# Two-block transformer forward on one Trainium2 core: bias and forget tables on GpSimd's DMA queue, query weights loaded ahead of the compressed branch's, first squares on ScalarE, output tiles j and j+4 in one PSUM bank

## The chip, the cores and the metric

The kernel runs as one program on one core of a Trainium2 chip. The metric is the device time of one execution in microseconds (us), as the median of several runs. TensorE (PE) multiplies, its weight loads (PEld) overlap with it; VectorE (DVE) and ScalarE (ACT) work element by element and empty PSUM; GpSimd (POOL) does small sums and reciprocal roots; SyncE (SP) issues most DMA transfers. DMA transfers can also be issued from POOL's own instruction stream, where they stand in line with its other instructions.

## What is computed

A sequence of 256 positions with 1,024 channels goes through two layers and then a second block of three stages, all in float32.

```
h = x
h = h + moba_nsa_mixer(rmsnorm(h))      # layer 0: dense causal heads with relative bias, and three-branch heads
h = h + sqrelu_mlp(rmsnorm(h))          # 1024 -> 4096 -> 1024
h = h + fox_mixer(rmsnorm(h))           # layer 1: 16 heads, forget gates
h = h + sqrelu_mlp(rmsnorm(h))
h = rmsnorm(h)
n = modulate(rmsnorm(h)); h = h + 0.5*gt1*swiglu(n)     # 2816 hidden
n = modulate(rmsnorm(h)); h = h + gt2*hybrid_mixer(n)   # pooling (4 windows) and dilated attention (8 heads)
n = modulate(rmsnorm(h)); h = h + 0.5*gt3*swiglu(n)
out = rmsnorm(h)

fox_mixer:  q, k, v, fz = split(h @ w_in);  log_f = log_sigmoid(fz + b_forget);  cum = cumsum(log_f over positions)
            s = q k^T * scale + cum[query] - cum[key];  p = causal softmax(s);  out = (p v) @ w_out
moba_nsa:   in 8 heads s = q k^T * scale + table[bucket(distance)], causal softmax, p v
            in 8 heads the same bias with three branches: compressed keys (silu(blocks @ w1) @ w2), selected, window
```

## The kernel before

Activations are held transposed: `Ht` is 128 partitions x 8 channel tiles x 256 positions. Float32 precision is kept by splitting each operand into a rounded high part and a remainder, so every product is three matmuls (`mm3`, lines 403 to 405: high x high, high weight x low activation, low weight x high activation). The activations' parts are `nh` and `nl`, the weights' `wh` and `wl`. A "product" below is one such group of three on a 128 x 128 weight tile.

**Weights.** `specs` lists all weight pieces (most are 1 MB) in the order in which they are loaded. They go into a ring of five raw buffers (`raw`): piece i+5 is loaded when piece i has been split. The split is done by halves, the high part by an ACT copy (L276, for the first piece L287) and the low part by a DVE subtraction (L282, first piece L288), into rings of five (`wh`, `wl`). Pieces of the compressed branch (`cmp`) are used as they are loaded. All these loads, the 786 KB write of the relative-bias table to DRAM (`vd`) and the eight reads of the table back from there (`hh<-vd`, 256 KB each, four for each of the tables `T[1]` and `T[0]`) stand in SP's stream one behind the other, through `queue()`, which keeps their order.

**Order of the work.** The kernel is written as a stream of projections. At certain points `poke()` runs one step of side work: hooks set with `later(n, f)` (f runs n pokes on), generators for attention (`quad`: scores `s` L749, bias and row minimum on DVE L759/L760, exponentials on ACT L761/L763, scaling on DVE L775/L776, transposes `t` on PE L783, their copy on ACT L785, products with v into `o` L807/L810), the splits of coming weights, and the modulation's row sums. `settle(key)` steps until the generators pushed under a key are done. Each engine then runs its instructions strictly in the order that comes out of this, so one that waits holds up all behind it on its engine.

**Norms.** Each stage begins projecting before its norm is known; the reciprocal root follows in three steps set by `norm_begin(eps, n1, n2)`: at poke n1 the sums of squares are reduced on PE (`ss`), at n2 the diagonal matrix is made, at n2+1 PE spreads it (`r`).

**First norm.** The squares of the input's eight tiles are summed by `first_squares`: for half of them POOL squares and adds (L533, L542, L547), for the other half ACT squares (L539) and DVE adds.

**Fox mixer.** The chunks of four heads come in the order c = 3, 2, 1, 0, each with projections fv, fq, fk. `forget` (in chunk 3) makes log_f, transposes it on PE (`a` L1304), sums it along the positions (DVE L1307), writes it to DRAM (`cd`, POOL L1310) and reads it back into all partitions in four parts for four heads each (`hh<-cd`, POOL L1312); then POOL adds the causal mask to the four parts (L1316), and for each head POOL adds it once more to a half (`pre`, L1339).

**Output projections.** `out_proj` and the second half of `ffn` collect eight output tiles of 128 x 256 in four PSUM banks, two tiles in each bank. Tiles 2t and 2t+1 share a bank:

```
ps = acc[t]                                  # ffn
mm3(ps[:, jj * S:(jj + 1) * S], ...)         # tile 2t+jj
ps = acc[2 * c + jj // 2]                    # out_proj, tile 4c+jj
```

When a tile is finished, DVE adds it to `Ht` (L868 in the first two mixers, L942/L943 in the MLPs, L1449 in the gated MLPs, L1551 in the hybrid mixer), and the next stage's `nh`, `nl` are made of it. During the last pair of tiles `state["hold"]` keeps the splits of coming weights back.

**Hybrid mixer.** v is transposed on PE by `v_trans` (`a` L1523), the pooled groups come from `pool_gen` (a chain of DVE additions L1492 to L1498, then `a` L1503 on PE); both are generators with fixed delays in pokes.

Of the kernel before, what the change touches and what calls it, by code (L numbers as in the profile page):

```python
# [19 lines left out]
P = 128  # L20
S = 256
# [47 lines left out]
def tile_two_blocks(ctx, tc, a, out):  # L69
# [166 lines left out]
    cap = [5]  # L236
# [84 lines left out]

    def take(name):
        i = state["next"]
        state["next"] += 1
        assert specs[i][0] == name, (specs[i][0], name)
        return Weights(i)
# [128 lines left out]
    def late_loads():  # L455
        for h in range(2):
            queue(w2k[:, :, 64 * h:64 * h + 64], rows(a["cmp_k_w2"], 0, 2))
        queue(w2v, rows(a["cmp_v_w2"], 0, 2))
# [68 lines left out]
    def first_squares(t):  # L527
        x = [Ht[:, 2 * t + j, :] for j in range(2)]
        if t < 2:
            eng = gp_  # L530
            sq = sb([P, 512], F32, "sq")
            for j in range(2):
                eng.tensor_tensor(sq[:, j * S:(j + 1) * S], x[j], x[j], OP.mult)  # L533
        else:
            eng = dve
            sq = sb([P, 512], F32, "ev", 3)
            with tc.issue_after(state["conva"]):
                for j in range(2):
                    act.activation(sq[:, j * S:(j + 1) * S], x[j], AF.Square)  # L539
        if t % 2 == 0:  # L540
            acc = sb([P, S], F32, ("ssq", "nv")[t // 2])
            eng.tensor_tensor(acc, sq[:, :S], sq[:, S:], OP.add)  # L542
            cur.setdefault("ssq", []).append(acc)
        else:
            acc = cur["ssq"][-1]
            for j in range(2):
                eng.tensor_tensor(acc, acc, sq[:, j * S:(j + 1) * S], OP.add)  # L547
# [270 lines left out]
    def out_proj(name, oh, ol, k0, swap, done):  # L818
        acc = [None] * 4

        def part(c, k0, first):
# [6 lines left out]
            def product(jj, h):  # L828
                ps = acc[2 * c + jj // 2]
                s = slice(jj * P, (jj + 1) * P)  # L830
                for i, k in enumerate(order[h]):
                    st = first and h == 0 and i == 0 and jj % 2 == 0
                    mm3(ps[:, jj % 2 * S:(jj % 2 + 1) * S], w.h(2 * h + i, s), w.l(2 * h + i, s), oh[:, k0 + k, :],
                        ol[:, k0 + k, :], st, not first and h == 1 and i == 1, skip_group_check=True)

            def out(jj):
                ps = acc[2 * c + jj // 2]
                done(4 * c + jj, ps[:, jj % 2 * S:(jj % 2 + 1) * S])
                if jj % 2:
# [21 lines left out]
        for c in range(2):  # L861
            part(c, k0, True)
        settle("o")
# [7 lines left out]
    def ffn(tag, n, up, done, hold=True):  # L871
# [3 lines left out]
        for i in range(len(bl) + 1):  # L875
# [10 lines left out]
            for t in range(4):  # L886
                w = take(tag + "2")
                if b == 0:
                    acc[t] = bank("acc")
                ps = acc[t]  # L890
                end = b == len(bl) - 1
                def part(jj, ks):
                    s = slice(jj * P, (jj + 1) * P)
                    for k in ks:
                        mm3(ps[:, jj * S:(jj + 1) * S], w.h(k, s), w.l(k, s), hh[:, k, :], hl[:, k, :],
                            b == 0 and jj == 0 and k == 0, end and k == m - 1, skip_group_check=True)
                    poke()
                if end and t == 3:
                    state["hold"] = hold
                    ks = [w.half(h) for h in range(2)]  # L900
                    for jj in range(2):
                        for x in ks:
                            part(jj, x)
                        done(2 * t + jj, ps[:, jj * S:(jj + 1) * S])
                    drop(ps)
# [5 lines left out]
                if end:  # L911
                    for j in range(2):
                        done(2 * t + j, ps[:, j * S:(j + 1) * S])
                    drop(ps)
# [72 lines left out]
    def body():  # L987
# [297 lines left out]
        norm_begin(1e-5, 4, 7)  # L1285
# [3 lines left out]
        def forget(ps):  # L1289
# [11 lines left out]
            yield 3  # L1301
            p = bank("a")
# [11 lines left out]
            for x in (3, 2, 1, 0):  # L1314
                part = cumb[x // 2][:, 4 * (x % 2):4 * (x % 2) + 4, P:S]
                gp_.tensor_tensor(part, part, tri[:, None, :].to_broadcast([P, 4, P]), OP.add)  # L1316
        oh_ = sb([P, KT, 258], F32R, "nh", 2)[:, :, :S]
        ol_ = sb([P, KT, 258], F32R, "nl", 2)[:, :, :S]
        for c in (3, 2, 1, 0):
            first = c == 3  # L1320
            q, k, v = qkv()
            if first:
                ps_v = gemm_nat_more("fv")

# [3 lines left out]
                on_norm(put_v)  # L1328
                ps_q = gemm_pair("fq")
                on_norm(lambda: evac_q(ps_q, q))  # L1330
            else:
                evac_v(gemm_nat("fv"), v)
                evac_q(gemm_pair("fq"), q)
            evac_k(gemm_pair("fk"), k)
            bts = {}

            def pre(j, e, t, c=c, bts=bts):
# [3 lines left out]
            push("o" if c < 2 else "f", quad(  # L1341
                q, lambda j, e, k=k: k[64 * e:64 * e + 64, j, :],
                lambda j, e, b, v=v: v[:, b, 128 * j + 64 * e:128 * j + 64 * e + 64],
                lambda j, e, bts=bts: bts[j, e],
                None, Out(oh_, ol_, 2 * c), True, pre, quick=c == 0), None)
        settle("f")
        new_n()
        out_proj("fout", oh_, ol_, 4, True, lagged(gain["mlp1"], add_h))
# [136 lines left out]
        def pool_gen(gi, u):  # L1485
# [13 lines left out]
            yield 2  # L1499
# [27 lines left out]
        for c in range(2):  # L1527
# [18 lines left out]
            on_norm(attend)  # L1546
# [99 lines left out]
```

## Time and profile before

| what | value |
|---|---|
| median of three runs | 1148.22 us (1147.53 to 1151.86) |
| the profiled execution, its own time | 1150.76 us |
| its span in the trace | 1149.0 us |
| PE busy | 1095.1 us, 95% of the span, 9,088 matmuls |
| PEld busy | 1064.0 us (93%) |
| DVE busy | 805.9 us (70%) |
| ACT busy | 577.1 us (50%) |
| POOL busy | 112.2 us (10%) |
| moved by DMA | 233.72 MB, mean 203 GB/s |

The shares are means over stages with different limits. A row of the timeline gives start, duration, engine, line, operation, output and inputs and, in brackets, how long the engine had been idle before and what released it. Matmuls overlap in the pipeline, so a matmul's own duration (0.28 us) is longer than the distance to the next one.

### The profile page before, as it was taken

How to read it: one execution, taken by the hardware profiler on the slowest of the kernel's cores; microseconds unless marked ns; L12 is line 12 of the kernel's file. 1: busy time of each engine (PE TensorE's matmuls, PEld its weight loads, DVE VectorE, ACT ScalarE, POOL GpSimd, SP SyncE). 2: the span in 40 equal slices, each digit the busy share in tenths (PEclk: the TensorE clock that was granted, in tenths of full speed). 3: DMA queues.
4: the chain of work that ended last, by engine and by line, in shares of the span. 5: the costliest groups of instructions: out<-in, count | busy, mean ns of one | idle time of the engine just before them, and what ended most of it. 6: DMA issues, size and time to landing. Idle time of an engine off the chain costs nothing.

```text
span 1149.0 us, 22404 instructions
## 1 busy us (share of the span) xinstructions
PE 1095.1 (95%) x9088; PEld 1064.0 (93%) x9088; DVE 805.9 (70%) x1534; ACT 577.1 (50%) x963; POOL 112.2 (10%) x150
## 2 busy tenths in 40 slices
PE   8689999999998699999999999999999899999997
PEld 8668899999997699999999999999998889999997
DVE  6577679787875465798878678756577867775654
ACT  5375566454445455554544565444355356444432
POOL 3010030000012310310000220000010012000001
PEclk9899999999999899999999999999999999999998
DMA  9962459999866344499999656565455456656521
GB/s 243 317 214 81 147 161 335 325 316 308 293 222 197 134 147 146 135 316 322 306 306 294 184 149 191 183 185 184 153 168 184 120 138 180 188 184 184 175 84 37
DMA packets 243752, 233.72 MB, mean 203 GB/s; under 512 B 6385, under 2 KB 227217, under 8 KB 243649
## 3 DMA queue, kind: packets, MB, share of 16 engines
q1 hardware_dynamic: 242304, 229.37, 63.8%
q0 software_dynamic: 768, 2.31, 0.6%
q8 instruction: 71, 1.16, 0.4%
q10 hardware_dynamic: 576, 0.62, 0.2%
q14 instruction: 33, 0.26, 0.1%
HBM read 230.42 MB, written 1.85 MB: 202 GB/s over the span
## 4 chain that ended last, share of the span: by engine, by line
PE 77%; DVE 9%; ACT 6%; DMA 4%; issue 2%; POOL 1%; SPq 0%; POOLq 0%; ACTq 0%; DVEq 0%
PE g L404 14%; PE g L403 14%; PE g L405 14%; PE acc L404 10%; PE acc L403 10%; PE acc L405 10%; DVE wl L282 3%; ACT wh L276 2%; DMA raw<-in_even_w_in_dram 1%; ACT sb L763 1%; PE s L749 1%; DMA vd<-ev 1%; PE t L783 1%; ACT sb L761 1%; DMA raw<-in_mlp_w_dram 1%
## 5 line engine op out<-in xcount | busy, mean ns | idle before, releaser
L282 DVE TENSOR_TENSOR wl<-raw,wh 128x1024 fp32r<-128x1024 f32 (+2 forms) x352 | 421.9, 1206 | 188.2 <-ACT wh L276 187.7
L276 ACT ACTIVATE wh<-raw 128x1024 fp32r<-128x1024 f32 (+2 forms) x352 | 362.1, 1036 | 308.7 <-PE acc L404 151.8
L405 PE MATMUL g<-nh,wl 128*128 128x258 f32 (+1 forms) x1600 | 453.0, 283 | 6.0 <-DVE wl L282 3.5
L403 PE MATMUL g<-nh,wh 128*128 128x258 f32 (+1 forms) x1600 | 455.8, 285 | 0.0
L404 PE MATMUL g<-nl,wh 128*128 128x258 f32 (+1 forms) x1600 | 452.4, 283 | 0.8 <-DVE nl L956 0.5
L405 PEld LDWEIGHTS g<-nh,wl 128*128 128x128 f32 x1600 | 303.1, 190 | 7.1 <-DVE wl L282 4.1
L403 PEld LDWEIGHTS g<-nh,wh 128*128 128x128 f32 x1600 | 303.7, 190 | 3.3 <-issue 3.2
L404 PEld LDWEIGHTS g<-nl,wh 128*128 128x128 f32 x1600 | 303.8, 190 | 2.5 <-DVE nl L956 2.0
L404 PE MATMUL acc<-hl,wh 128*128 128x256 f32 x864 | 246.1, 285 | 0.0
L403 PE MATMUL acc<-hh,wh 128*128 128x256 f32 x864 | 241.1, 279 | 2.7 <-DVE H L1449 2.2
L405 PE MATMUL acc<-hh,wl 128*128 128x256 f32 x864 | 241.5, 279 | 0.0
L403 PEld LDWEIGHTS acc<-hh,wh 128*128 128x128 f32 x864 | 162.4, 188 | 3.4 <-DVE H L1449 2.6
L404 PEld LDWEIGHTS acc<-hl,wh 128*128 128x128 f32 x864 | 162.4, 188 | 0.0
L405 PEld LDWEIGHTS acc<-hh,wl 128*128 128x128 f32 x864 | 162.2, 188 | 0.0
L483 DVE SCALAR_TENSOR_TENSOR ada<-ada,cb 128x1024 f32<-128x1024 f32 x72 | 88.4, 1229 | 14.0 <-DMA ada<-in_w_adaT_dram 13.5
L507 POOL TENSOR_TENSOR ssq<-sq 128x256 f32<-128x256 f32 x7 | 9.0, 1288 | 828.6 <-ACT sq L518 828.6
L403 PE MATMUL acc<-nh,wh 128*128 128x256 f32 x192 | 55.9, 291 | 1.6 <-DVE H L868 1.0
L404 PE MATMUL acc<-nl,wh 128*128 128x256 f32 x192 | 53.9, 281 | 0.0
L405 PE MATMUL acc<-nh,wl 128*128 128x256 f32 x192 | 53.9, 281 | 0.0
L1441 ACT ACTIVATE ev<-ev,bb 128x256 f32<-128x256 f32 x44 | 22.2, 509 | 59.0 <-DVE ev L1438 59.0
L783 PE MATMUL t<-cst,sb 128*128 128x128 f32 x144 | 26.7, 294 | 21.1 <-DVE sb L775 13.8
L511 POOL TENSOR_TENSOR ssq<-ssq,sq 128x256 f32<-128x256 f32 x40 | 39.0, 976 | 49.4 <-ACT sq L518 48.1
(229 smaller groups left out, 1095.0 us busy)
## 6 DMA issues: line engine op xcount, KB each, us to landing
raw<-in_mlp_w_dram SPq DMA_DIRECT2D x64, 1024.0 KB, 7.2
ada<-in_w_adaT_dram SPq DMA_DIRECT2D x72, 512.0 KB, 6.1
raw<-in_w_gate_dram SPq DMA_DIRECT2D x44, 512.0 KB, 4.0
raw<-in_w_up_dram SPq DMA_DIRECT2D x44, 512.0 KB, 5.2
raw<-in_w_down_dram SPq DMA_DIRECT2D x16, 1024.0 KB, 5.2
raw<-in_odd_w_in_dram SPq DMA_DIRECT2D x11, 1024.0 KB, 5.4
raw<-in_even_w_in_dram SPq DMA_DIRECT2D x8, 1024.0 KB, 7.6
raw<-in_w_in_dram SPq DMA_DIRECT2D x8, 1024.0 KB, 5.7
```

The lines of the kernel that those rows point to most:

```text
L276: state["conva"] = act.activation(his[u], r[0], AF.Copy).ins
L282: state["conv"] = dve.tensor_tensor(los[u], r[0], his[u].bitcast(F32), OP.subtract).ins
L403: pe.matmul(ps, wh, xh, start=start, stop=False, **kw)
L404: pe.matmul(ps, wh, xl, start=False, stop=False, **kw)
L405: state["mm"] = pe.matmul(ps, wl, xh, start=False, stop=stop, **kw).ins
L483: dve.scalar_tensor_tensor(t, t, 1.0, cb, op0=OP.mult, op1=OP.mult, accum_out=modT[:, i:i + 1])
L511: gp_.tensor_tensor(acc, acc, sq[:, j * S:(j + 1) * S], OP.add)
L749: pe.matmul(ps[j, e][:, c], q[s, j, b * P:(b + 1) * P], k_of(j, e)[:, 0:P + P * b], start=True, stop=True)
L761: act.activation(x[:, 0:P], x[:, 0:P], AF.Exp, scale=-1.0, bias=mn[:, 0:1], accum_out=rr[j][:, 2 * e:2 * e + 1])
L763: act.activation(x[:, P:384], x[:, P:384], AF.Exp, scale=-1.0, bias=mn[:, 1:2], accum_out=rr[j][:, 2 * e + 1:2 * e + 2])
L783: pe.transpose(p[:, c * P:(c + 1) * P], t[j, e][:, c * P:(c + 1) * P], ident)
L1441: act.activation(t[:, :S], t[:, :S], AF.Silu, bias=bb[:, 0:1])
```

## The change

- The write of the bias table and the eight reads of it are issued by POOL instead of SP, as are the three small loads of `late_loads`; the second table's reads come six pokes later than the write in program order. Loads of weights are no longer capped at five until the table is written.
- In `specs` the first query piece (`mq`) stands ahead of the four compressed pieces instead of behind them; `take` now looks pieces up by name.
- `first_squares`: all squares on ACT; POOL adds the first four tiles, DVE the last four.
- Fox mixer: the norm's steps at pokes 2 and 5 instead of 4 and 7; the forget chain starts one poke after fv instead of after the norm; the mask is added to one part ahead of chunk 3 and to the others as their chunks come; chunk 3's attention is pushed five pokes later; waits on chunks by their own keys.
- `out_proj` and `ffn`: tiles that share a bank are j and j+4 in the MLPs (jj and jj+2 in a half of the output projections); `hold` is set for the last tile alone.
- Hybrid mixer: `pool_gen` yields 4 instead of 2, `v_trans` starts after 3 pokes instead of 1, attention 2 pokes later.

```
     for c in range(2):
         spec_cols("mv", we, 1024 + 256 * c)
+        spec_cols("mq", we, 256 * c)
         if c == 0:
             for w in ("cmp_k_w1", "cmp_v_w1"):
                 for h in range(2):
                     spec("cmp", [(0, rows(a[w], 8 * h, 8))], 8, 256, True)
-        spec_cols("mq", we, 256 * c)
         spec_cols("mk", we, 512 + 256 * c)
...
-    cap = [5]
+    cap = [len(specs)]
...
     def first_squares(t):
-        x = [Ht[:, 2 * t + j, :] for j in range(2)]
-        if t < 2:
-            eng = gp_
-            sq = sb([P, 512], F32, "sq")
+        if t % 2 == 0:
+            cur["sq"] = sb([P, 4, S], F32, ("cb", "ada")[t // 2], 1 + t // 2)
+        sq = cur["sq"]
+        with tc.issue_after(state["conva"]):
             for j in range(2):
-                eng.tensor_tensor(sq[:, j * S:(j + 1) * S], x[j], x[j], OP.mult)
...
+                act.activation(sq[:, 2 * (t % 2) + j, :], Ht[:, 2 * t + j, :], AF.Square)
+        if t % 2:
+            eng = (gp_, dve)[t // 2]
...
             def product(jj, h):
-                ps = acc[2 * c + jj // 2]
+                ps = acc[2 * c + jj % 2]
...
+                def half(jj):
+                    j = 2 * t + jj
+                    return acc[j % 4][:, j // 4 * S:(j // 4 + 1) * S]
...
                 if end and t == 3:
-                    state["hold"] = hold
                     ks = [w.half(h) for h in range(2)]
                     for jj in range(2):
+                        if jj:
+                            state["hold"] = hold
...
         def read_table(x):
             for b in range(4):
-                queue(T[x].rearrange("(a b) h f -> b a h f", b=4)[b],
+                gp_.dma_start(T[x].rearrange("(a b) h f -> b a h f", b=4)[b],
...
-            queue(vd.rearrange("a h j -> h a j"), vexp[:, None, :].to_broadcast([16, 32, 384]))
-            read_table(1)
-            cap[0] = len(specs)
-            load_to(cap[0])
+            gp_.dma_start(vd.rearrange("a h j -> h a j"), vexp[:, None, :].to_broadcast([16, 32, 384]))
+            later(6, lambda: read_table(1))
...
-        norm_begin(1e-5, 4, 7)
+        norm_begin(1e-5, 2, 5)
...
-            for x in (3, 2, 1, 0):
-                part = cumb[x // 2][:, 4 * (x % 2):4 * (x % 2) + 4, P:S]
-                gp_.tensor_tensor(part, part, tri[:, None, :].to_broadcast([P, 4, P]), OP.add)
+            mask(3)
+
+        def mask(x):
+            part = cumb[x // 2][:, 4 * (x % 2):4 * (x % 2) + 4, P:S]
+            gp_.tensor_tensor(part, part, tri[:, None, :].to_broadcast([P, 4, P]), OP.add)
...
-                on_norm(put_v)
+                later(1, put_v)
...
+            if first:
+                later(5, attend)
+            else:
+                attend()
+        settle(("f", 3))
+        settle(("f", 2))
...
-            yield 2
+            yield 4
             while not space(1):
...
-                go(v_trans(vt, v, j), 1)
+                go(v_trans(vt, v, j), 3)
...
-            on_norm(attend)
+            on_norm(lambda attend=attend: later(2, attend))
```

SP's stream at the start, from the load of the last of the first five pieces; `raw` are weight buffers, `vd` the bias table in DRAM, `hh` its copies in SBUF. Before:

```order
L214 DMA raw<-in_even_w_in_dram 128x8x256
L214 DMA vd<-ev 16x32x384
L214 DMA hh<-vd 32x8x256 x4
L214 DMA raw<-in_even_w_in_dram 128x8x256 x2
L214 DMA raw<-in_cmp_k_w_dram 128x8x256 x2
L214 DMA raw<-in_cmp_v_w_dram 128x8x256 x2
L214 DMA raw<-in_even_w_in_dram 128x8x256
```

SP's stream at the same place now:

```order
L214 DMA raw<-in_even_w_in_dram 128x8x256 x4
L214 DMA raw<-in_cmp_k_w_dram 128x8x256 x2
L214 DMA raw<-in_cmp_v_w_dram 128x8x256 x2
L214 DMA raw<-in_even_w_in_dram 128x8x256 x4
```

The table's write and its four first reads are gone from between the weights, and one more piece of `even_w_in` (the query piece) is ahead of the compressed ones. POOL's stream at the start now (`ssq` are sums of squares, the rows on `nat` are the reciprocal root of the first norm; before, no DMA stood here):

```order
L539 TENSOR_TENSOR ssq<-cb 128x256
L1025 DMA vd<-ev 16x32x384
L541 TENSOR_TENSOR ssq<-ssq,cb 128x256 x2
L560 TENSOR_TENSOR nat<-nat,mhalf 128x2
L561 TENSOR_TENSOR nat<-nat 128x2
L562 TENSOR_TENSOR nat<-nat 128x2
L563 TENSOR_SCALAR nat<-nat 128x2
L564 TENSOR_TENSOR nat<-nat 128x2
L1015 DMA hh<-vd 32x8x256 x4
L459 DMA w2k<-in_cmp_k_w_dram 128x2x64 x2
L460 DMA w2v<-in_cmp_v_w_dram 128x2x64
L1015 DMA hh<-vd 32x8x256 x4
```

The reads wait in POOL's stream for the write to land, behind the norm's reciprocal root. DVE's stream in the fox mixer, from the cumulative sum of the forget gates (`ev<-ev,a`) to the first bias additions of chunk 3 (`sb,mn<-s,...`; `hl<-g` rows take projections out of PSUM). Before:

```order
L1307 SCALAR_TENSOR_TENSOR ev<-ev,a 16x256
L282 TENSOR_TENSOR wl<-raw,wh 128x1024
L707 TENSOR_TENSOR hl<-g,rbc 128x512
L759 ISA sb,mn<-s,sb 128x128
L759 ISA mn 128x1
L760 ISA sb,mn<-s,hh 128x256
```

The same place now:

```order
L1311 SCALAR_TENSOR_TENSOR ev<-ev,a 16x256
L282 TENSOR_TENSOR wl<-raw,wh 128x1024
L698 SCALAR_TENSOR_TENSOR hl<-g,rbc 128x512
L282 TENSOR_TENSOR wl<-raw,wh 128x1024 x2
L702 TENSOR_TENSOR hl<-g,rbc 128x512
L282 TENSOR_TENSOR wl<-raw,wh 128x1024 x2
L754 ISA sb,mn<-s,sb 128x128
L754 ISA mn 128x1
L755 ISA sb,mn<-s,hh 128x256
```

Five splits of coming weights instead of one stand between the sum and the first addition that needs its copy; on PE, 52 products instead of 24 stand between the transposes `a` of the forget gates and the first transposes `t` of chunk 3's attention, and the 16 score matmuls `s` are in both. POOL's stream there, before:

```order
L1310 DMA cd<-ev 16x256
L1312 DMA hh<-cd 128x1024 x4
L1316 TENSOR_TENSOR hh<-hh,cst 128x4x128 x4
L1339 TENSOR_TENSOR sb<-hh,cst 128x128 x16
L507 TENSOR_TENSOR ssq<-sq 128x256
```

POOL's stream there now:

```order
L1314 DMA cd<-ev 16x256
L1316 DMA hh<-cd 128x1024 x4
L1322 TENSOR_TENSOR hh<-hh,cst 128x4x128
L1349 TENSOR_TENSOR sb<-hh,cst 128x128 x4
L1322 TENSOR_TENSOR hh<-hh,cst 128x4x128
L1349 TENSOR_TENSOR sb<-hh,cst 128x128 x4
```

One mask addition instead of four is ahead of the first `sb` that chunk 3 needs.

## Rows read from the trace of the kernel before

**Rows 1.** Busy time by stretch: stretch, length, busy us (instructions) per engine, clock, DMA.
```profile
16.53:128.47 111.94, 97.58 (x845) 85.92 (x845) 75.49 (x241) 58.65 (x153) 7.03 (x16) 0.97 0.64 198
128.47:342.67 214.20, 212.51 (x1781) 209.40 (x1780) 167.47 (x245) 109.17 (x158) 17.36 (x18) 1.00 0.83 273
342.67:445.48 102.81, 88.24 (x718) 83.59 (x717) 56.25 (x128) 53.28 (x109) 23.74 (x31) 0.93 0.48 154
855.69:917.30 61.61, 55.78 (x452) 52.54 (x451) 47.75 (x125) 30.44 (x53) 3.49 (x6) 1.00 0.44 138
```

**Rows 2.** PE's waits in all: us in total, times, longest.
```profile
PE g L405 <- DVE wl L282: 3.5, 3, 1.8
PE a L1503 <- DVE sb L1498: 2.8, 3, 1.2
...
PE acc L403 <- DVE H L1449: 2.2, 2, 1.6
PE a L1523 <- DVE ev L1483: 1.7, 3, 0.9
PE s L749 <- DVE hl L1483: 1.3, 1, 1.3
...
PE acc L403 <- DVE H L868: 1.0, 2, 0.5
...
PE acc L403 <- DVE H L1551: 0.6, 1, 0.6
PE acc L403 <- DVE ev L942: 0.5, 1, 0.5
```

**Rows 3.** Chain that ended last, at the start: start, duration, what.
```profile
14.56 10.68 DMA vd<-ev
...
28.00 7.62 DMA raw<-in_even_w_in_dram
```

**Rows 4.** Timeline of layer 0's first attention, ACT, DVE and PE.
```profile
30.30 2.36 DVE L282 TENSOR_TENSOR wl<-raw,wh 128x1024 fp32r<-128x1024 f32 x2
...
35.70 2.01 ACT L276 ACTIVATE wh<-raw 128x1024 fp32r<-128x1024 f32 x2 [7.91 <-DMA raw<-in_even_w_in_dram]
...
40.95 0.28 DVE L759 CUSTOM_DVE_ANT_0 sb<-s,hh 128x128 f32<-128x128 f32 x1
...
48.90 0.91 PE L783 MATMUL t<-cst,sb 128*128 128x128 f32 x3 [7.10 <-issue]
```

**Rows 5.** Busy time of three short stretches, columns as in rows 1.
```profile
49.46:52.17 2.71, 2.71 (x15) 2.71 (x14) 1.32 (x7) 0.00 (x0) 0.00 (x0) 0.50 1.07 361
387.29:389.99 2.70, 2.70 (x14) 2.70 (x13) 2.32 (x8) 2.40 (x5) 1.51 (x1) 0.50 0.03 1
403.50:405.01 1.51, 1.51 (x17) 1.13 (x16) 0.44 (x3) 0.11 (x1) 0.00 (x0) 1.00 0.80 298
```

**Rows 6.** Timeline of the fox mixer, PE's rows that waited.
```profile
361.52 0.39 PE L1304 MATMUL a<-cst,ev 128*16 128x128 f32 x2 [0.22 <-DVE ev L1298]
368.28 2.93 PE L749 MATMUL s<-hl 64*128 64x128 f32 x16 [3.51 <-DVE hl L707]
386.76 0.87 PE L783 MATMUL t<-cst,sb 128*128 128x128 f32 x3 [9.64 <-DVE sb L775]
```

**Rows 7.** Timeline of the fox mixer, POOL and DVE.
```profile
370.40 2.12 POOL L1312 DMA_DIRECT2D hh<-cd  x4 [2.98 <-PE s L749]
375.04 1.29 POOL L1316 TENSOR_TENSOR hh<-hh,cst 128x512 f32<-128x512 f32 x1 [2.51 <-DMA hh<-cd]
377.58 3.78 POOL L1316 TENSOR_TENSOR hh<-hh,cst 128x512 f32<-128x512 f32 x3 [1.25 <-DMA hh<-cd]
...
381.81 0.29 DVE L759 CUSTOM_DVE_ANT_0 sb<-s,sb 128x128 f32<-128x128 f32 x1 [13.59 <-POOL sb L1339]
```

**Rows 8.** Timeline of the first piece, ACT and PE.
```profile
11.03 0.71 ACT L539 ACTIVATE ev<-H 128x256 f32<-128x256 f32 x2
...
16.53 0.39 PE L405 MATMUL g<-nh,wl 128*128 128x256 f32 x1 [0.59 <-DVE wl L282]
```

More of the change, by code (lines that the diff above doesn't have):

```diff
@@ L320, in l @@
             return los[unit[self.i, k // self.n]][:, k % self.n, s]
+    taken = set()
     def take(name):
-        i = state["next"]
-        state["next"] += 1
-        assert specs[i][0] == name, (specs[i][0], name)
+        i = next(x for x in range(len(specs)) if x not in taken and specs[x][0] == name)
+        assert all(x in taken or specs[x][4] != specs[i][4] for x in range(i)), name
+        taken.add(i)
         return Weights(i)
@@ L456, in late_loads @@
         for h in range(2):
-            queue(w2k[:, :, 64 * h:64 * h + 64], rows(a["cmp_k_w2"], 0, 2))
-        queue(w2v, rows(a["cmp_v_w2"], 0, 2))
+            gp_.dma_start(w2k[:, :, 64 * h:64 * h + 64], rows(a["cmp_k_w2"], 0, 2))
+        gp_.dma_start(w2v, rows(a["cmp_v_w2"], 0, 2))
     modT = sb([P, 72], F32, "modT")
@@ L862, in out_proj @@
             part(c, k0, True)
+        settle(("f", 1))
         settle("o")
@@ L887, in ffn @@
                 w = take(tag + "2")
-                if b == 0:
-                    acc[t] = bank("acc")
-                ps = acc[t]
                 end = b == len(bl) - 1
+                if b == 0 and t < 2:
+                    acc[2 * t:2 * t + 2] = [bank("acc") for _ in range(2)]
+                def half(jj):
+                    j = 2 * t + jj
+                    return acc[j % 4][:, j // 4 * S:(j // 4 + 1) * S]
                 def part(jj, ks):
@@ L894, in part, with out @@
                     for k in ks:
-                        mm3(ps[:, jj * S:(jj + 1) * S], w.h(k, s), w.l(k, s), hh[:, k, :], hl[:, k, :],
-                            b == 0 and jj == 0 and k == 0, end and k == m - 1, skip_group_check=True)
+                        mm3(half(jj), w.h(k, s), w.l(k, s), hh[:, k, :], hl[:, k, :],
+                            b == 0 and t < 2 and k == 0, end and k == m - 1, skip_group_check=True)
                     poke()
+                def out(jj):
+                    done(2 * t + jj, half(jj))
+                    if t > 1:
+                        drop(acc[(2 * t + jj) % 4])
                 if end and t == 3:
-                    state["hold"] = hold
                     ks = [w.half(h) for h in range(2)]
                     for jj in range(2):
+                        if jj:
+                            state["hold"] = hold
                         for x in ks:
                             part(jj, x)
-                        done(2 * t + jj, ps[:, jj * S:(jj + 1) * S])
-                    drop(ps)
+                        out(jj)
                     continue
@@ L911, in ffn @@
                 if end:
-                    for j in range(2):
-                        done(2 * t + j, ps[:, j * S:(j + 1) * S])
-                    drop(ps)
+                    for jj in range(2):
+                        out(jj)
     def mlp(layer, nextfeed):
@@ L1301, in forget @@
             yield 3
+            while len(spare) < 2:
+                yield 1
             p = bank("a")
@@ L1320, in body @@
             first = c == 3
-            q, k, v = qkv()
             if first:
                 ps_v = gemm_nat_more("fv")
+                q, k, v = qkv()
                 def put_v():
@@ L1331, in body @@
             else:
-                evac_v(gemm_nat("fv"), v)
+                ps = gemm_nat("fv")
+                settle(("f", c + 2))
+                q, k, v = qkv()
+                evac_v(ps, v)
                 evac_q(gemm_pair("fq"), q)
+                mask(c)
             evac_k(gemm_pair("fk"), k)
```

38 lines of the change are left out of this document (15 added, 23 removed).

## The prediction

> **What bounds the kernel now.** I read the busy time by stretch first [rows 1]. In the MLP stretch from 128 to 343 us PE starts 1,781 matmuls in 214.20 us, one each 0.120 us, and nothing is lost: there the kernel is bound by its matmuls, and the change takes none away. The other stretches fall short of that pace. From 16.5 to 128.5 us 845 matmuls need 101.4 us and take 111.94: 10.5 lost. The fox mixer's 718 need 86.2 and take 102.81: 16.6 lost. The hybrid mixer's 452 need 54.2 and take 61.61: 7.4 lost. So the change is worth what it gives back of these 34.5 us, and of some short waits at the stages' ends. PE runs in order, so second I read who ends its waits [rows 2, 4, 6], and third, behind each, the chain that made the releaser late [rows 3, 7].
>
> One thing more is to be seen there. After a long wait PE runs at the lower of its clock's two levels for a while: 12 matmuls of three products took 2.71 us after the first wait and 2.70 after the last, at a granted clock of 0.50, where the pace gives 1.44 [rows 5]. So a wait costs more than its length.
>
> **Layer 0's attention: the table off SP's queue, and the query piece's place.** SP issues the table's write at 14.56 and its landing takes 10.68 us [rows 3]; the reads behind it wait for it, the weights behind the reads too. The next weight piece is issued only at 28.00 and lands 7.62 us later. ACT stands idle 7.91 us for it, the attention's first bias addition on DVE comes at 40.95, the first transposes on PE at 48.90, after an idle time of 7.10 [rows 4].
> With the table on POOL's queue this piece is issued as soon as its buffer is free. DVE is done with the pieces ahead of it at 32.66 (30.30 + 2.36), where before it got the first high half at 36.7 (35.70 and half of 2.01). So at most 4.0 us are gained up to the first transposes. The bound from below: the same DMA engines now carry the write and the reads beside the weights, and if the weights lose all of that share, the piece comes hardly earlier than before: 0. I take 2.7, nearer to the upper end, because in the old order SP's queue had nothing to send between the write's packets and the reads. A shorter wait (about 4.4 instead of 7.1) shortens the slow restart too, by about 1. The query piece no longer stands behind four compressed pieces; that is within what the stretch still loses, 10.5 less 7.1 and the restart's 2, and I give it 1.3. Sum 5, bounds 0 and 9.
> The Trainium skill (DMA: Bandwidth & Descriptors, SWDGE vs HWDGE vs iDMA) says that a DMA engine round-robins between the software and the hardware queues. By that the weights loaded at 15 to 25 us lose half their share to the table while it is written, which is the lower bound's side; no row here shows two full queues side by side.
>
> **First squares on ScalarE.** Four squares move from POOL to ACT, 0.36 us each [rows 8], 1.4 us on ACT before its first whole piece. What hides them is that piece's landing: PE's first matmul on it waits at 16.53 for its low half. I take 0; without that cover it would cost 1.4, and at best the 0.6 of that wait is gained.
>
> **The fox mixer.** From the forget gates' transposes `a` (361.52) to chunk 3's first transposes `t` (386.76) 25.2 us pass [rows 6]. PE has 24 products of three matmuls (8.6 us) and 16 score matmuls (1.5 us at full clock [rows 5]) to do in them, 10.2 us: 15.1 are lost, in the waits of 3.51 and 9.64 and in scores that took 2.93. The chain behind it: sum, write, read back (first read issued at 370.40, landed at 375.04), then all four masks (375.04 to 381.36) before the first bias addition at 381.81 [rows 7].
> Now three masks (3.78) are behind the first use, so the chain is at most 21.5 us long, and PE has 52 products and the scores in it: 18.7 + 1.5 = 20.2 us. What is late next is at most 1.3 us at `t`. DVE has five splits between the sum and the bias addition instead of one; they fall into its 13.59 us of waiting for POOL. The wait for k's evacuation (3.51) goes, since 16 products of the next chunk's v and 4 more lie between. The slow stretch behind `t` (1.3 in the row, about 2 in all) goes as well. Against the stretch's whole loss of 16.6 plus what the row's count hides I take 16.5. Upper bound 18 (15.1, the restart's 2 and the longest wait for a weight split at its start, about 1, of the 3.5 in rows 2). Lower bound 13: the reads back now share the DMA engines with weight loads that SP could not issue before; one more 1.3 us for each of the first two reads, and the 1.3 above.
> The norm's steps two pokes earlier cost nothing while ss, root and r have 16 products between them (5.8 us).
>
> **Tiles j and j+4.** PE waited at the end of stages for DVE to read the other half of the bank that it wants to write: 2.2 + 1.0 + 0.6 + 0.5 = 4.3 us in six waits [rows 2]. These rows count from a matmul's modelled end, 0.28 after its start, where the next could start after 0.12, so 0.16 more each: 5.3. The next tile now lies in another bank, whose reader was asked one tile earlier (1.4 us). I take 5. Bounds 2 (the wait moves to the next stage's first use of the last `nh` and `nl`) and 5.3. Two banks less are free at a stage's end; that hides behind the last products, and would cost a bank's evacuation if a new stage wanted a fifth.
>
> **The hybrid mixer.** Its seven waits are 2.8 + 1.7 + 1.3 = 5.8 us, 6.9 with the 0.16 each [rows 2]. The pool's matmuls move behind 4 more products (1.45 us), chunk 1's transposes behind 8, the scores behind 4; the longest waits were 1.2, 0.9 and 1.3. But DVE is busy for 47.75 of the 61.61 us [rows 1]; with 6.9 less it would be busy for 87%, and what it does not finish earlier PE will still wait for. I take 4, bounds 2.5 and 6.9.
>
> **Sum.** 5 + 0 + 16.5 + 5 + 4 = 30.5 us, from the profiled execution's 1150.76 (1149.0 span and 1.8 around it): 1120.3. That execution is 2.5 above the median of the runs, so I forecast 1118. The bounds give 17.5 to 39.2, so 1131 to 1109.
>
> **Rivals.**
> *Tables crowd the weights.* POOL writes and reads the table while the pieces for 22 to 30 us are still coming, and a piece late there delays ACT's copy of r, which stands behind its split. For it: the engines' share in that time leaves little room. Against it: the pieces landed some us before their use. It would take back the 5 and up to 2 more: 1123 to 1125.
> *The forget chain is still late.* If write and read back take 5 us longer beside weight loads, `t` waits 6 and the clock falls again for 1 to 2: 1125 to 1126. Against it: the chain's length is 21.5 with nothing taken off.
> *The bank was not the reason.* If DVE was simply behind, PE meets the same wait one tile later: 3 to 5 back, 1121 to 1123, the same with the hybrid mixer's DVE.
> *Tables come too late, slower than before.* The eight reads wait in POOL's stream, and chunk 0's attention waits for them. Each us that the first table lands after about 38 delays the first transposes by one; the change as a whole is lost when it lands after 38 + 30 = 68, and slower by 0.5% (5.7 us) from 74. For it: nothing in the trace shows POOL issuing 256 KB reads of 1 KB rows. Against it: POOL issued four reads of twice that size in 2.12 us, and the masks behind them all ran by 381.4, 11 us after the first issue [rows 7]. At twice 11 us from 23 it would be 45, 7 us late, 1125; I price the mechanism at 1148 to 1160.
> The Trainium skill (SBUF — State Buffer, SBUF: two separate sides) has a rule on the side of this rival: while DVE runs an operation in a two-port mode, GpSimd cannot write descriptors, and its DMAs starve. By its section on who interferes with whom tensor_tensor has no such mode; DVE's rows between 30 and 41 us are of that kind, so by the rule too the sum stays. No run here shows such a DMA under a two-port operation.
>
> **How the numbers follow.** The forecast 0.63, its own range 1111 to 1125. Tables crowd 0.13, forget chain 0.10, bank or DVE 0.06, tables too late 0.08. All but the last are faster by far more than 0.5% (5.7 us, about what a measurement of this kernel can tell from no change); of the last, 0.03 falls within 0.5% and 0.05 is slower. The range 1109 to 1133 leaves out the last and some of the edges.
>
> **What would show it.** Right: the next weight piece issued near 14 us and ACT's 7.9 us of idle time gone; first transposes of chunk 0 at 44 to 47 with 3 to 5 us of waiting; the fox mixer from its first product to the output projection's first in 85 to 88 us, with no PE wait over 2; no `acc` wait on DVE over 0.3; hybrid waits of 2 to 4 us in all. Wrong: a first table that lands after 38; a wait of several us at chunk 3's `t`, or a low clock behind it; waits on H that reappear on `nl`; a new wait of ACT on the second key piece, which is now the last in the ring.

## The result and the profile after

The changed kernel takes 1117.16 us (median of 4 runs, 1113.91 to 1118.57) against 1148.13 before: a ratio of 0.972, 95% interval 0.9688 to 0.9751. The forecast was 1118. The profiled execution took 1118.57 with a span of 1116.8. So the sum came out, but not term by term: the experiments show that layer 0's gain had another cause than the one I gave it, that the output tiles and their hold gave more than I said and the fox and hybrid mixers less. In one kernel below (chunk 3's attention not put off) one of five executions took 2113.57 us and is left out of its ratio.

First, the busy time of the stretches that answer to [rows 1] and [rows 5]: the same matmuls, found by their number in PE's order. Columns as there; the last stretch is the one after the first transposes.

```profile
17.19:124.34 107.15, 96.16 (x844) 85.01 (x845) 74.88 (x241) 58.26 (x153) 13.76 (x27) 0.98 0.66 205
124.34:335.94 211.60, 211.10 (x1780) 209.04 (x1779) 168.12 (x246) 109.58 (x160) 15.04 (x17) 1.00 0.83 276
335.94:422.61 86.67, 84.74 (x719) 80.41 (x718) 56.71 (x128) 53.24 (x109) 24.71 (x32) 1.00 0.55 183
828.36:887.15 58.79, 56.20 (x452) 54.29 (x451) 48.25 (x127) 29.16 (x54) 4.56 (x8) 0.97 0.48 154
48.83:51.40 2.57, 2.57 (x15) 2.57 (x14) 2.50 (x8) 0.49 (x1) 0.00 (x0) 0.53 1.10 349
```

Against before, the first stretch is 4.8 us shorter, the MLP with the end of the attention 2.6, the fox mixer 16.1, the hybrid mixer 2.8. The last row is the slow restart: 15 matmuls in 2.57 us at a granted clock of 0.53, so it is still there behind layer 0's first transposes. PE's waits, in total, times and longest, against [rows 2]:

```profile
PE t L778 <- DVE sb L770: 5.0, 7, 2.0
PE t L778 <- issue: 4.7, 1, 4.7
PE g L407 <- DVE wl L282: 3.9, 2, 3.1
PE s L744 <- DVE hl L702: 1.5, 2, 1.3
...
PE s L744 <- DVE hl L1501: 0.6, 1, 0.6
```

No row with `acc` is left, and none with the pooled or transposed `a`. The longest wait for a weight split, 3.1 us, is in layer 0 (at 33.48) and was 1.8 before. Against [rows 4] and [rows 7], the timeline of ACT and PE in layer 0, then of POOL and PE in the fox mixer:

```profile
27.42 1.06 ACT L276 ACTIVATE wh<-raw 128x1024 fp32r<-128x1024 f32 x1 [3.27 <-DMA raw<-in_even_w_in_dram]
...
33.73 2.01 ACT L276 ACTIVATE wh<-raw 128x1024 fp32r<-128x1024 f32 x2 [4.03 <-DMA raw<-in_even_w_in_dram]
...
40.34 1.06 ACT L276 ACTIVATE wh<-raw 128x1024 fp32r<-128x1024 f32 x1 [3.32 <-DMA raw<-in_even_w_in_dram]
...
48.42 0.66 PE L778 MATMUL t<-cst,sb 128*128 128x128 f32 x3 [4.70 <-issue]
...
356.52 2.13 POOL L1316 DMA_DIRECT2D hh<-cd  x4 [3.28 <-issue]
363.92 1.28 POOL L1322 TENSOR_TENSOR hh<-hh,cst 128x512 f32<-128x512 f32 x1 [5.27 <-DMA hh<-cd]
...
370.63 0.61 PE L778 MATMUL t<-cst,sb 128*128 128x128 f32 x3 [0.94 <-DVE sb L770]
```

In the fox mixer the 9.64 us wait of `t` is down to 0.94. In layer 0 ACT no longer waits once for 7.91 us but three times for 10.6 us in all, and `t` comes at 48.42, hardly earlier than before (48.90). The piece whose late issue (28.00) I had blamed is issued at 14.61 now and lands at 33.65, 2 us earlier than its 35.62 before.

### The profile page after: what moved, and what is told of

Its sections match the earlier page's. It is cut to its first block, busy times and chain, and to the rows that moved or that the text cites. A ratio compares the mean times of both kernels' runs of the same rounds, so it can differ in the third digit from the quotient of the medians.

```text
span 1116.8 us, 22415 instructions
## 1 busy us (share of the span) xinstructions
PE 1087.8 (97%) x9088; PEld 1061.7 (95%) x9088; DVE 809.1 (72%) x1534; ACT 578.1 (52%) x967; POOL 115.4 (10%) x158
## 4 chain that ended last, share of the span: by engine, by line
PE 80%; DVE 6%; ACT 5%; DMA 5%; issue 2%; POOL 1%; SPq 0%; POOLq 0%; ACTq 0%; DVEq 0%
PE g L405 15%; PE g L407 15%; PE g L406 15%; PE acc L406 10%; PE acc L405 10%; PE acc L407 10%; DMA raw<-in_even_w_in_dram 3%; DVE wl L282 2%; ACT wh L276 2%; DMA ada<-in_w_adaT_dram 1%; PE t L778 1%; ACT sb L758 1%; PE s L744 1%; PE o L802 1%; ACT sb L756 1%
## 5 line engine op out<-in xcount | busy, mean ns | idle before, releaser
L405 PEld LDWEIGHTS acc<-nh,wh 128*128 128x128 f32 x192 | 36.3, 189 | 2.1 <-issue 1.5
```

What stands on the lines that cost most here:

```text
L405: pe.matmul(ps, wh, xh, start=start, stop=False, **kw)
```

## The experiments

All ratios are to the kernel before on the same chip. The changed kernel stands at 0.972, and at 0.9713 (0.9693 to 0.9733) when it was run again; I take 0.9717. A difference from it times 1149.5 us, about before's median in these runs, is the price of an edit, known to some 2 us. Finer is the trace: PE's 9,088 matmuls are compared by their number, so that a loss has a place; "by the trace" means that, against the profile of the run again.

**The changed kernel again.**

> The changed kernel itself once more, since its own runs lie between 1113.9 and 1118.6 us and half of the parts are smaller than that. If the first profile stood for it, 1117 to 1118 and a ratio of 0.972; if, as the other kernels' profiles suggest, layer 0 mostly goes some 2 us better than in that profile, 1115 to 1116 and 0.970 to 0.971.

1116.46 us (1115.89 to 1119.1). The first transposes come at 47.95 after a wait of 2.10 here, and at 48.42 after 4.70 in the first profile: layer 0 differs from execution to execution. By how much, eight kept traces tell, these two and six of the runs below that leave layer 0's stream up to its output projection as it is (fox mixer, masks, attention, banks, hold, hybrid delays): their matmul 800 starts between 108.45 and 111.66 us. It comes before matmul 300 and between 400 and 500; from 300 to 400 the eight take 11.06 to 11.11 us, from 500 to 800 34.52 to 34.57.

**The tables back on SP's queue.**

```diff
-    cap = [len(specs)]
+    cap = [5]
...
-                gp_.dma_start(T[x].rearrange(...)[b], ...)
+                queue(T[x].rearrange(...)[b], ...)
...
-            gp_.dma_start(vd.rearrange("a h j -> h a j"), ...)
-            later(6, lambda: read_table(1))
+            queue(vd.rearrange("a h j -> h a j"), ...)
+            read_table(1)
+            cap[0] = len(specs)
+            load_to(cap[0])
```

> The changed kernel with the table's write and its reads on SP's queue again and the loads capped at five until then; the query piece stays ahead of the compressed ones. Theory (the queue was what made the pieces late): 3 to 5 us slower, 1120 to 1122, and the first transposes of chunk 0 at 50 us or later instead of 48.4. Rival (the DMA engines were full anyway and the tables only move the wait): within 1.5 us of the changed kernel, first transposes within 1 us of 48.4.

1117.91 us, 0.9727 (0.9713 to 0.9742): 1.1 us, not to be told from nothing; by the trace it is 0.4 us ahead at matmul 800. The rival was right. The timeline shows ACT's long wait back, and PE hardly later for it:

```profile
35.59 2.00 ACT L276 ACTIVATE wh<-raw 128x1024 fp32r<-128x1024 f32 x2 [7.92 <-DMA raw<-in_even_w_in_dram]
...
48.79 0.45 PE L778 MATMUL t<-cst,sb 128*128 128x128 f32 x1 [5.56 <-issue]
```

Why, the DMA view of 13.5 to 45 us shows in 40 slices: busy share of the 16 engines in tenths, and GB/s. First the changed kernel, then the one with the tables on SP's queue:

```profile
DMA  9999999999869999999999999999999999999999
GB/s 294 305 303 324 302 222 127 131 114 107 99 152 382 384 376 347 350 361 351 346 360 362 334 286 277 308 350 365 352 343 358 317 347 365 332 339 346 347 349 350
```

```profile
DMA  9999999998998762059999799999999999999999
GB/s 295 314 299 310 337 350 345 358 397 113 119 107 101 121 157 99 0 96 349 333 295 277 208 342 351 362 372 371 352 345 351 351 342 354 342 346 349 355 334 341
```

While the table is written, the engines move little: 107 to 131 GB/s in the slices in which they are full with it, about 350 once weights or reads fill them again. On SP's queue the engines are partly or wholly idle towards the end of the write and behind it, 2 to 3 us in all, and that is what the move to POOL's queue could give. On POOL's queue two things take it back. The weights get next to nothing while the table is written, as the two queues show in the changed kernel from 18.4 to 21.4 us (q0 is POOL's, q1 SP's; packets, MB, share of the 16 engines):

```profile
q0 software_dynamic: 65, 0.30, 96.0%
q1 hardware_dynamic: 25, 0.02, 2.2%
```

And the second table's 1 MB comes in among the weights; the run with these reads later, below, prices that. The same four 1 MB pieces land at 20.6, 35.5, 38.5 and 42.0 us with the tables on SP's queue, at 27.3, 33.7, 40.3 and 43.7 with them on POOL's.

**The query piece behind the compressed ones again.**

```diff
-        spec_cols("mq", we, 256 * c)
         if c == 0:
             ...
+        spec_cols("mq", we, 256 * c)
         spec_cols("mk", we, 512 + 256 * c)
```

> The changed kernel with the query piece behind the four compressed pieces again; the tables stay on POOL's queue. After the run with the tables back on SP's queue cost nothing, the theory is that layer 0's gain is the query piece's: it would land at 53 to 56 us again instead of 43.7, its split would hold up ACT and DVE there, and PE would wait some 3 us at 62 to 66: 2.5 to 4 us slower than the changed kernel, ratio to before 0.974 to 0.976. Rival (the piece's place is nearly free, as my 1.3 us said): 0 to 1.5 us, 0.972 to 0.9735.

1122.0 us, 0.9764 (0.9745 to 0.9782): 5.4 us, and 4.1 by the trace at matmul 800. Somewhat above what the theory gave, far above my 1.3. The place is sharp: from matmul 300 to 400 this kernel takes 15.43 us, where the eight traces take 11.06 to 11.11, and from 500 to 800 35.52, where they take 34.52 to 34.57: 5.3 us in the two stretches that otherwise hardly vary. Timeline, ACT and PE:

```profile
54.48 1.06 ACT L276 ACTIVATE wh<-raw 128x1024 fp32r<-128x1024 f32 x1 [9.19 <-DMA raw<-in_even_w_in_dram]
...
55.97 0.39 PE L405 MATMUL g<-wh,nh 128*128 128x256 f32 x1 [1.07 <-ACT pt L780]
...
64.88 0.33 PE L778 MATMUL t<-cst,sb 128*128 128x128 f32 x1 [1.61 <-DVE sb L770]
```

ACT waits 9.19 us for the piece; the copies of `t` out of PSUM, DVE's half of the split and everything that DVE does for the attention stand behind it. Of the 4.3 us of the first stretch, 1.3 are lost at 55.97, where PE waits for such a copy, and 2.8 at the waits between 62 and 65 us.

**The second table's reads later.** `late_loads()` and `read_table(0)` move behind POOL's additions for the compressed branch:

```diff
-        late_loads()
-        read_table(0)
         ps_c = gemm_pair("kcvc")
         ...
         gp_.tensor_copy(Cb[:, :, 1, :], T[1][:, :, 31:256:16])
+        late_loads()
+        read_table(0)
```

> The changed kernel with the four reads of the second table (1 MB) and the three small loads moved in POOL's stream behind the compressed branch's additions, so to 60 us instead of 26 to 33. Theory (the DMA engines are full from 13 to 56 us, and bytes decide when a piece lands): the pieces that land at 40.3 and 43.7 us land 2.5 to 3.5 us sooner, the first transposes come 1.5 to 3 us sooner, 1114 to 1115.5, ratio 0.9695 to 0.971. Rival (SP's rows go first and the table's reads only fill gaps): landings within 0.7 us, ratio 0.972.

1114.17 us, 0.9688 (0.9673 to 0.9703): 3.3 us faster than the changed kernel, 4.1 by the trace at matmul 800. The two pieces land at 35.9 and 38.9, where the changed kernel's two profiles have 40.3 and 43.7, 39.8 and 42.8: about 4 us sooner, even more than expected. ACT's waits shrink, and `t` with them:

```profile
27.00 1.06 ACT L276 ACTIVATE wh<-raw 128x1024 fp32r<-128x1024 f32 x1 [1.44 <-DMA raw<-in_even_w_in_dram]
31.31 2.00 ACT L276 ACTIVATE wh<-raw 128x1024 fp32r<-128x1024 f32 x2 [1.45 <-DMA raw<-in_even_w_in_dram]
...
46.49 0.65 PE L778 MATMUL t<-cst,sb 128*128 128x128 f32 x3 [2.61 <-issue]
```

So while the engines are full, the bytes ahead of a piece decide when it lands, not the time at which it is issued.

**First squares of before.** `first_squares` as in the kernel before.

```diff
+        if t < 2:
+            eng = gp_
...
+                eng.tensor_tensor(sq[:, j * S:(j + 1) * S], x[j], x[j], OP.mult)
...
-                act.activation(sq[:, 2 * (t % 2) + j, :], Ht[:, 2 * t + j, :], AF.Square)
...
```

> The changed kernel with the first squares of before (half of them squared and added on POOL). Prediction's step: nothing, since the first piece's landing hides ACT's 1.4 us; the profile of the changed kernel stands 0.66 us behind at the 75th matmul. Theory (hidden): within 1 us, ratio 0.971 to 0.973. Rival (POOL's squares also hold up the table's write, which now stands in POOL's stream): 1 to 3 us slower, ratio 0.973 to 0.975.

1115.39 us, 0.9704 (0.9688 to 0.972): 1.5 us faster than the changed kernel, inside the uncertainty; by the trace 2.1 us ahead at matmul 800, just outside the eight traces (108.09 us). The rival's time is excluded, but what it named happens: the table's write goes out later, at 14.31 us instead of 12.59 to 13.57 in the eight traces. That goes with a 1 MB piece next to it that lands at 25.68 instead of 26.32 to 27.66. ACT's copy of `r` stands behind that piece's split, and DVE's next work behind that copy:

```profile
26.84 0.39 ACT L585 ACTIVATE rbc<-r 128x256 f32<-128x256 f32 x1
```

In the changed kernel's first profile this row is at 28.39 (L578). PE's wait for a low half at matmul 178 is 1.83 here and ends at 31.96; in the eight traces it ends between 32.96 and 33.82.

**Both together** (the reads later and the first squares of before).

> The changed kernel with the second table's reads moved behind the compressed branch's additions, which gave 3.7 us, and the first squares of before, which gave 1.8 us that a measurement can hardly tell from nothing. If the squares' part is real, ratio 0.967 to 0.9685 and below the run with the reads alone; if not, 0.9685 to 0.970.

1112.55 us, 0.9671 (0.9652 to 0.9691), the fastest version here: 2.0 us better than the reads alone. Twice, then, the old squares are 1.5 to 2 us better, each time inside the interval. The trace again has matmul 178 early, at 31.88 instead of 33.65 with the reads alone, so up to there a cost of about 1 us of the squares on ScalarE is shown. How much of it is left at the end is not: at matmul 800 this trace is 0.3 us behind that of the reads alone.

**The fox mixer of before.** The stretch from `norm_begin` to `out_proj` and the extra settle are those of the kernel before.

```diff
-        norm_begin(1e-5, 2, 5)
+        norm_begin(1e-5, 4, 7)
...
-                later(1, put_v)
+                on_norm(put_v)
```

> The changed kernel with the fox mixer of before (norm steps, forget chain, four masks at once, attention not put off). Theory: the 9.6 us wait at chunk 3's first transposes and the 3.5 us wait at its scores come back with the half clock behind them, 16 to 17 us, so 1133 to 1135. Rival (part of that loss came from the bank and the tables of the stages before): 10 to 13 us, 1127 to 1130.

1130.22 us, 0.9832 (0.9818 to 0.9847): 13.2 us, 13.5 by the trace from matmul 2700 to 3400, the mixer itself. Below the theory, just above the rival's range. In the kernel before, the same matmuls lose 17.5 us. Of the 4.0 between the two, 1.8 are at the mixer's start (matmuls 2700 to 2800), where before PE waits 1.06 for a weight split and here it does not; the hold alone, below, acts there. The rest goes with shorter waits of `s` and `t` (2.38 and 8.90 instead of 3.51 and 9.64), the cause of which is not shown. `t` waits again, for 8.90 us:

```profile
374.35 0.87 PE L778 MATMUL t<-cst,sb 128*128 128x128 f32 x3 [8.90 <-DVE sb L770]
```

**All four masks at once.**

```diff
-            mask(3)
+            for x in (3, 2, 1, 0):
+                mask(x)
...
-                mask(c)
```

> The changed kernel with all four mask additions ahead of chunk 3's first addition again; nothing else moves. Theory (chunk 3's first transposes still wait for the chain, by 1.2 us, so all that is put into it shows): the fourth part lands 4.9 us after the first, the first bias addition comes 4.9 us later, PE waits 5 to 6 us more at t and starts slowly behind it: 5 to 6.5 us slower than the changed kernel. Rival (the products put ahead cover it): under 1.5 us.

1123.65 us, 0.9771 (0.9753 to 0.9789): 6.2 us, as the theory had it. POOL's rows show that not the masks' own 1.3 us each but the landings of the four reads set it; then PE's wait, and the stretch behind it at half clock (columns as in rows 1):

```profile
361.92 1.26 POOL L1323 TENSOR_TENSOR hh<-hh,cst 128x512 f32<-128x512 f32 x1 [3.74 <-DMA hh<-cd]
364.89 1.27 POOL L1323 TENSOR_TENSOR hh<-hh,cst 128x512 f32<-128x512 f32 x1 [1.70 <-DMA hh<-cd]
366.58 1.29 POOL L1323 TENSOR_TENSOR hh<-hh,cst 128x512 f32<-128x512 f32 x1 [0.42 <-DMA hh<-cd]
368.31 1.29 POOL L1323 TENSOR_TENSOR hh<-hh,cst 128x512 f32<-128x512 f32 x1 [0.44 <-DMA hh<-cd]
...
375.00 0.66 PE L778 MATMUL t<-cst,sb 128*128 128x128 f32 x2 [5.51 <-DVE sb L770]
...
375.53:378.24 2.71, 2.71 (x15) 2.71 (x14) 2.33 (x6) 1.80 (x3) 1.52 (x1) 0.50 0.01 2
```

**Chunk 3's attention not put off.**

```diff
             if first:
-                later(5, attend)
+                attend()
             else:
                 attend()
```

> The changed kernel with chunk 3's attention not put off by five pokes: 36 products instead of 52 stand between the forget gates' transposes and the first t. Theory (PE's cover is what counts): 16 products, 5.8 us, are missing, and the scores wait for k's evacuation again: 5.5 to 7.5 us slower. Rival (the masks' place was the gain and the products matter little): under 2 us.

1122.59 us, 0.9758 (0.974 to 0.9776): 4.7 us, somewhat under the theory's range and well above the rival's. `t` waits 4.35 us, at 368.94, instead of 0.94 in the changed kernel's first profile and no such wait in its second. The chain itself differs by as much: its first read lands at 362.1 here, at 363.8 and 361.7 in those two.

**Banks and hold of before.** `product`, `out` and the second half of `ffn` are those of before:

```diff
-                ps = acc[2 * c + jj % 2]
+                ps = acc[2 * c + jj // 2]
...
+                    state["hold"] = hold
...
-                        if jj:
-                            state["hold"] = hold
```

> The changed kernel with tiles 2t and 2t+1 in one bank again and hold set for the last pair. Theory (PE waited for the reader of the other half of its bank): the six waits of acc for DVE at the stages' ends come back, 0.6 to 1.8 us each, 5 to 7 us in all, so 1122 to 1124 and a ratio to before of 0.977 to 0.979. Rival (DVE was simply behind, and PE met the same wait one tile later): under 2 us, 1117 to 1119.

1127.58 us, 0.9811 (0.9796 to 0.9826): 10.8 us, 10.2 by the trace from matmul 800 on. The rival is out, but the theory is half of it. The waits of `acc` are back at their old size, 4.4 us in six. Two more waits for a weight's low half, 0.66 and 2.08 us at 341 and 350 us, are at the start of the fox mixer, where this trace loses 4.0 us (matmuls 2700 to 2800; the longest of the first row, 2.7, is layer 0's):

```profile
PE g L407 <- DVE wl L282: 5.5, 3, 2.7
...
PE acc L405 <- DVE H L1459: 2.2, 2, 1.6
...
PE acc L405 <- DVE H L864: 1.0, 2, 0.5
PE acc L405 <- DVE H L1561: 0.7, 1, 0.7
PE g L406 <- DVE wl L282: 0.7, 1, 0.7
...
PE acc L405 <- DVE ev L938: 0.5, 1, 0.5
```

**Hold alone of before**, the banks as changed.

```diff
+                    state["hold"] = hold
...
-                        if jj:
-                            state["hold"] = hold
```

> The changed kernel with the splits held back during the last pair of tiles in the feed-forward stages, as before, and the banks as changed. Undoing banks and hold together cost 10 us, twice the waits for a bank. Theory (the other half is the next stage's weights, split late because of the hold: there PE waited 1.0 and 2.4 us for a low half at the start of the fox mixer): 3 to 5 us slower than the changed kernel, ratio 0.975 to 0.9765, with waits of g for DVE wl at the stages' starts. Rival (all of the 10 us comes from the banks): under 1 us.

1118.58 us, 0.9728 (0.971 to 0.9746): 1.3 us by the runs, so the theory's 3 to 5 is not confirmed there. The profiled execution (1121.38, near the top of 1116.52 to 1121.76) shows the mechanism: 4.0 us at the start of the fox mixer, as in the trace with banks and hold of before:

```profile
349.86 0.51 PE L407 MATMUL g<-nh,wl 128*128 128x256 f32 x1 [2.06 <-DVE wl L282]
```

With the hold the first pieces of the fox mixer are split later, a raw buffer is free later, SP issues the next piece at 341.92 instead of 338.86 in the changed kernel's first profile, and it lands at 347.4 instead of 344.2 (0.9 of the difference is older: it stands at matmul 2700 already). Both traces with this hold show it; the five runs together give 1.3 us, known to some 2, so what it costs in most executions is not settled. At the six waits for a bank this trace and that with banks and hold of before part by 6.6 us; the banks were not undone alone.

**The hybrid mixer's delays of before** (2, 1 and 0 pokes).

```diff
-            yield 4
+            yield 2
...
-                go(v_trans(vt, v, j), 3)
+                go(v_trans(vt, v, j), 1)
...
-            on_norm(lambda attend=attend: later(2, attend))
+            on_norm(attend)
```

> The changed kernel with the hybrid mixer's delays of before (2, 1 and 0 pokes instead of 4, 3 and 2). Theory (PE's order was the reason for its short waits): 2.5 to 3 us slower, 1120, with the waits of a on DVE back. Rival (DVE is the bound of that stretch, the waits only change places): under 1 us.

1118.57 us, 0.9729 (0.9713 to 0.9745): 1.4 us, 2.3 by the trace, with the waits of `a` back at 2.8 and 1.7 us as in [rows 2]. Between theory and rival, nearer to the theory by the trace. The wait of 1.96 us that the changed kernel has at the first transposes (860.07) is not there: part of the wait had only moved.

## Why the prediction was right, and where its steps were not

The five parts undone one by one cost 1.1 + 5.4 + 13.2 + 10.8 + 1.4 us, the squares give 1.5 back: 30.4, against the 32.5 that the change gave (0.0283 of 1149.5) and the 30.5 forecast. That the sum is this near is in part luck. The errors of the terms cancel, and the parts are not independent: the hold of before costs 4.0 us at the fox mixer's start in the two traces with it, but the kernel before lost only 1.0 there against the changed one. Step by step:

- **Layer 0, 5 us: right size, wrong cause.** The first step that failed is "if the weights lose all of that share, the piece comes hardly earlier than before: 0. I take 2.7". The lower bound held, and the sign that I had named, first transposes at 44 to 47, did not come (48.42 and 47.95). The first-named rival, tables that crowd the weights, is what happened, not as an addition to a gain but in place of it, and by the way it named: ACT's copy of `r` stands behind the split of a late piece. The Trainium skill (DMA: Bandwidth & Descriptors, SWDGE vs HWDGE vs iDMA) has a DMA engine taking turns between the two kinds of queue. The trace shows both queues moving at once, but not the half shares that I had made of it: 96.0% against 2.2%. The 1 MB piece next to the write took 7.7 us when the write stood behind it in SP's queue, and 13.7 with the write on POOL's queue, issued 0.2 us ahead of it. The second step that failed is the query piece at 1.3; it is worth 5.3 to 5.4. I had given it what the stretch's loss left over once 7.1 and the restart's 2 were booked to the table's wait, and did not look at what stands behind its split on ACT.
- **First squares, 0:** they are hidden at the first pieces, as I said (matmul 75 starts at 17.36 with the old squares, at 17.18 and 17.65 with the new). What I had not seen is that POOL's squares held the table's write back. By the runs 1.5 to 2 us of cost are likely, not shown.
- **Fox mixer, 16.5: mechanism right, size 13.2 to 13.5.** Masks and products both count, 6.2 and 4.7 us when one is undone. Of the remainder to the stretch's 16.1, up to 1.8 us go with the weight splits at its start, which I had booked here as "the longest wait for a weight split at its start"; the rest stays open. The stretch took 86.7 us where I said 85 to 88; `t` waits 0.94, inside the 1.3 allowed. Reads that land later beside weight loads are real: the first took 7.3 us from its issue, 6.1 in the second profile, where it took 4.6 in [rows 7], and DVE still waited for POOL.
- **Tiles j and j+4, 5: too small.** The waits for a bank are the size that I gave them (4.4, with 0.16 more each 5.3), and PE loses 6.6 at them by the trace. The line of the change that moves `hold` I had priced at nothing. It is 1.3 by the runs and 4.0 by two traces; what it is in most executions stays open, and so does how the 10.8 divide.
- **Hybrid mixer, 4: 1.4 to 2.8**, at my lower bound or under it. DVE did not get faster with PE: the attention's first transposes now wait 1.96 at 860.07, and the granted clock of the stretch is 0.97 instead of 1.00.

Of the rivals, "the bank was not the reason" and "the forget chain is still late" did not come. "Tables come too late" did not either: the fourth read of the first table landed at 33.4 us and DVE used it at 38.98. How much later it could have come was not tried. In that rival I read DVE's rows between 30 and 41 us as tensor_tensor throughout; they hold TENSOR_SCALAR and RECIPROCAL too, 1.25 us in all between 38.1 and 39.7. POOL's eight reads, issued at 23.77 to 32.63, landed 6 to 8 us later, none held up.

## What to carry to other kernels

When a queue seems to hold up a load, look at the engines' busy share first: where they were full, issuing earlier gained nothing here, and what helped was less or later traffic ahead of the piece, or another order of the pieces. Price a late load by the engine that stands in line for it and all that is queued behind that, not by the one wait in which it surfaces. A wait at a stage's end and a wait at the next stage's start can have one cause, here the same few lines; undo parts one at a time before booking them.

## What the runs showed of the hardware that was not expected

- Sixteen DMA engines at 90% busy or more moved about 350 GB/s with weights, but 107 to 131 GB/s while a 786 KB table was written to DRAM, in rows of 1.5 KB out of 16 partitions, whichever queue issued it. Which of these makes it slow was not tried.
- With such a write on POOL's queue beside weight loads on SP's, the engines' time did not go by halves: 96.0% went to the write and 2.2% to the weights.
- Behind short waits of 1 to 2 us a spell of half clock comes in some executions and not in others. With the reads later, PE waited 1.41 and 0.76 us at 14 to 17 us and then ran from 18.38 to 22.25 at a granted clock of 0.57; with the hybrid mixer's delays of before it waited 1.57 and 0.76 there and kept 1.00. PE's instructions of that stretch are the same. Of the nine traces in which PE waited 1.38 to 1.59 us at the first of these places, four have the spell and come to matmul 100 later by 1.2 to 1.6 us. It does not explain how layer 0 differs between executions: the run with the fox mixer of before has it and is the earliest of the eight at matmul 800. The two stretches, with the reads later and with the hybrid mixer's delays of before (columns as in rows 1):

```profile
18.38:22.25 3.87, 3.87 (x23) 3.87 (x22) 1.05 (x2) 1.34 (x2) 0.00 (x0) 0.57 0.95 112
```

```profile
18.00:20.00 2.00, 2.00 (x20) 2.00 (x18) 1.36 (x3) 0.00 (x0) 0.00 (x0) 1.00 1.05 112
```
